# Attention of a two-layer diffusion block: key tiles taken two at a time from a written plan, with the maxima of two heads side by side on the rows of TensorE

## The chip, the core and the metric

The kernel runs as one program on one core of a Trainium2 chip. Its time is the device time of one execution in microseconds (us). Several executions are made, and their median is the number to compare.

A core has TensorE (PE, matrix products into PSUM), VectorE (DVE), ScalarE (ACT), GpSimd (POOL) and SyncE (SP, which issues most transfers). Each engine works through its own instructions in order and waits where an operand or a buffer isn't ready.

## The reference

Two layers over 1024 tokens (and, in the first layer, 256 context tokens) of width 1024: a mixer of attention, short convolution and a recurrent unit, and then 16 experts, each of which picks its own tokens. The change lies in the attention alone:

```
def gqa_attend(q, k, v):
    s = jnp.einsum('bqhgd,bkhd->bhgqk', q, k, preferred_element_type=jnp.float32) * (HEAD_DIM ** -0.5)
    p = jax.nn.softmax(s, axis=-1).astype(v.dtype)
    return jnp.einsum('bhgqk,bkhd->bqhgd', p, v)
...
    k_all = jnp.concatenate([k_ctx, k_lat], axis=1)      # 256 + 1024 keys
    att_x = lax.map(lambda qb: gqa_attend(qb, k_all, v_all), q_blocks)   # 8 blocks of 128 queries
...
    att_c = gqa_attend(q_ctx, k_ctx, v_ctx)              # first layer only: 256 queries, 256 keys
```

There are 8 query heads of 64 channels on 2 key heads (kv 0 and 1, four query heads each). All inputs are float32.

## The kernel before

Each layer has four stages: projections with convolution and recurrence, attention, output projection with routing, experts. The attention of a layer is a stretch of some 230 to 250 us, in which the order of every instruction on PE, ACT, DVE and POOL is the order of the code.

**Query tiles and steps.** A query tile has 128 tokens with all 8 heads. It runs over 10 key tiles of 128 keys, and each of these is one *step*; the two context tiles of the first layer run over 2. That is 84 steps in the first layer and 80 in the second. One step (`scores`, lines 887 to 904) does this for each kv: two products of 512 columns into a PSUM tile `St` (L893 with the high halves of q and k, L894 with the low halves and the shift), an exponential by ACT into `PT` (L896), and an addition of `PT` to the running sum `acc` (L904). `St` has two buffers and `PT` has eight. The additions go to POOL for kv 0, and for kv 1 while the key tile's number is under `JP` = 4; the others go to DVE. Then `weigh` (L911) multiplies `PT` with V into `O`, for both kv, two steps late (`LAG` = 2). Its two products stand in the two halves of TensorE's columns.

**Preparation of the next tile.** The exponential needs the negative maximum of each query and head as a shift, before the tile's first step. `q_prep` is a generator of 16 pieces for a tile: four transposes into a PSUM tile `X` (L747) with ACT copies of the high half (L753, L756) and DVE differences for the low half (L758); then for each pair of heads two pieces with 2 products of 512 columns and a DVE maximum over 1024 columns (L769, L771), and one with 2 products of 256 columns and a maximum over 512 (L778, L780); then the negative (L797, L798); then a transpose of it (L803) and two DVE products that put it into the low half of q (L805). `X` has two buffers of 1024 columns. `advance` deals these pieces out evenly, one or two behind each kv of the steps.

**Late work.** A list `late` counts steps (`tick`) and holds the sums' reciprocals (`norm`, L919, `norm2`), and the splitting of the output projection's weights into halves: 32 parts of 256 columns, an ACT copy (L862) and a DVE difference (L863) each. From step 36 on, `w_out_unit` loads one of four weight blocks; the parts of a block follow at every second tick, and the blocks overlap, so that there come to be two parts for two steps. In the first 8 steps of a layer `filler` puts in products of the modulation (L159).

Of the kernel before, what the change touches and what calls it, by code (L numbers as in the profile page):

```python
# [8 lines left out]
F32 = mybir.dt.float32  # L9
# [35 lines left out]
def dit_kernel(ctx: ExitStack, tc: tile.TileContext, x, c, ctxt, c_ctx, w_mod, b_mod, norm1_g, norm2_g,  # L45
# [157 lines left out]
    JP, LAG, NL, NL1, NL2, LD, PB = 4, 2, 3, 2, 4, 2, 8  # L203
# [64 lines left out]
    for l in range(layers):  # L268
# [474 lines left out]
        def q_prep(tt, slot, xb, joint):  # L743
            nk = NTA if tt >= NTC else NTC
            b = xb()
            for p_ in range(4):
                pe.transpose(b[0][:, p_ * P:(p_ + 1) * P], qraw[:, tt, p_ * P:(p_ + 1) * P], ident)  # L747
            qq = slot()
            qh, ql = qq[:, 0:1024], qq[:, 1024:2048]
            v = lambda t: t.rearrange("p (h a t) -> p a h t", a=2, t=P)  # L750
            src = b[0].rearrange("p (h t) -> p h t", h=4)
            for a in range(2):
                act.activation(v(qh[0:64])[:, a], src[a * 64:a * 64 + 64], AF.Copy)  # L753
            yield
            for a in range(2):
                act.activation(v(qh[64:128])[:, a], src[a * 64:a * 64 + 64], AF.Copy)  # L756
            for a in range(2):
                vec.tensor_sub(v(ql[64:128])[:, a], src[a * 64:a * 64 + 64], v(qh[a * 64:a * 64 + 64])[:, a].bitcast(F32))  # L758
            mx = at_mx()
            yield  # L760
            np_ = 0
            if nk == NTA:
                for p_ in range(4):
                    ks = kst[p_ // 2]
                    hs = (2 * p_, 2 * p_ + 1)
                    for h in hs:
                        b = xb()
                        for i in range(2):
                            pe.matmul(b[i], qh[:, h * P:(h + 1) * P], ks[:, i * 512:(i + 1) * 512], start=True, stop=True)  # L769
                        if joint:  # L770
                            vec.tensor_reduce(mx[:, h, 0:1], b[2], axis=AX.X, op=OP.max)  # L771
                        else:
                            for i in range(2):
                                vec.tensor_reduce(mx[:, h, 2 * i:2 * i + 1], b[i], axis=AX.X, op=OP.max)
                        yield
                    b = xb()
                    for i, h in enumerate(hs):
                        pe.matmul(b[0][:, i * 256:(i + 1) * 256], qh[:, h * P:(h + 1) * P], ks[:, 1024:1280],  # L778
                                  start=True, stop=True)
                    vec.tensor_reduce(mx[:, hs[0]:hs[1] + 1, 1], b[0].rearrange("p (h k) -> p h k", h=2), axis=AX.X,  # L780
                                      op=OP.max)
                    np_ = 2 if joint else 3
                    yield
            else:
                for kv in range(2):
                    b = xb()
                    for i in range(4):
                        h = 4 * kv + i
                        pe.matmul(b[i // 2][:, (i % 2) * 256:(i % 2) * 256 + 256], qh[:, h * P:(h + 1) * P],
                                  kst[kv][:, 0:256], start=True, stop=True)  # L790
                    vec.tensor_reduce(mx[:, 4 * kv:4 * kv + 4, 0], b[2].rearrange("p (h k) -> p h k", h=4), axis=AX.X,
                                      op=OP.max)
                    np_ = 1
                    yield
            nm = nmx[len(tiles) % 2]
            if np_ > 1:
                vec.tensor_reduce(nm[:, 0:8], mx[:, :, 0:np_], axis=AX.X, op=OP.max)  # L797
# [3 lines left out]
            yield  # L801
            b = xb()
            pe.transpose(b[0][0:HD, 0:P], nm, ident)  # L803
            for kv in range(2):
                vec.tensor_mul(ql[0:HD, kv * 512:(kv + 1) * 512].rearrange("p (h t) -> p h t", h=4),  # L805
                               b[0][0:HD, None, 0:P].to_broadcast([HD, 4, P]),
                               ident[0:HD, 4 * kv:4 * kv + 4, None].to_broadcast([HD, 4, P]))
            tiles[tt] = (qh, ql, nk)
            yield
# [15 lines left out]
        first = q_prep(NTC, rslot, xb1, False)  # L825
# [55 lines left out]
        def xb2():  # L881
            t = pps.tile([P, 1024], F32, name="X", tag="X", bufs=2)
            return t[:, 0:512], t[:, 512:1024], t
# [4 lines left out]
        def scores(tt, j, kv):  # L888
# [7 lines left out]
            act.activation(pt, st, AF.Exp)  # L896
            if j == 0:
                return
# [5 lines left out]
            eng.tensor_add(a, PT[tt, 0, kv] if first_ else a, pt)  # L904
# [33 lines left out]
        cost = lambda t2: 16 if t2 >= NTC else 6  # L938
        rest = [q_prep(t2, qslot if t2 >= NTC else rslot, xb2, True) for t2 in order[1:]]
# [6 lines left out]
        done = [0]  # L946

        def advance(target):
            while done[0] < target:
                while rest and next(rest[0], "end") == "end":  # L950
                    rest.pop(0)
                done[0] += 1
# [10 lines left out]
        base = st_n = 0  # L963
        advance(LD)
        for g in groups:
            n_p = sum(cost(order[i + 1]) for i in g if i + 1 < len(order))
            n_s = sum(2 * tiles[order[i]][2] if order[i] in tiles else 2 * NTC for i in g)
            slot_ = 0
            for tt in (order[i] for i in g):
                for j in range(tiles[tt][2]):  # L970
                    for kv in range(2):
                        scores(tt, j, kv)
                        if kv:
                            lag.append((tt, j))
                            while len(lag) > LAG:
                                a, b = lag.pop(0)
                                weigh(a, b)
                                if b == tiles[a][2] - 1:
                                    late.append([NL, lambda a=a: norm(a)])
                            tick()  # L980
                        slot_ += 1
                        advance(base + LD + n_p * slot_ // n_s)
                    filler(1)
                    st_n += 1
                    if st_n in WS:
                        w_out_unit(WS.index(st_n))
            base += n_p
# [668 lines left out]
```

## Time and profile before

| | us |
|---|---|
| median of 3 runs | 2744.03 (2739.17 to 2745.43) |
| profiled execution, its own time | 2740.52 |
| its span, first to last instruction | 2738.7 |
| attention of the first layer, first score to last sum of a tile | 311.5 to 560.3 |
| attention of the second layer, up to its last sum of a tile | 1757 to 1987 |

Over the whole span PE is busy 95% of the time, DVE 73%, ACT 54% and POOL 27%. These are averages over unlike stages; the change concerns the two attention stretches, together some 480 us, and has to be read there.

### The profile page before, as it was taken

How to read it: one execution, taken by the hardware profiler on the slowest of the kernel's cores; microseconds unless marked ns; L12 is line 12 of the kernel's file. 1: busy time of each engine (PE TensorE's matmuls, PEld its weight loads, DVE VectorE, ACT ScalarE, POOL GpSimd, SP SyncE). 2: the span in 40 equal slices, each digit the busy share in tenths (PEclk: the TensorE clock that was granted, in tenths of full speed). 3: DMA queues.
4: the chain of work that ended last, by engine and by line, in shares of the span. 5: the costliest groups of instructions: out<-in, count | busy, mean ns of one | idle time of the engine just before them, and what ended most of it. 6: DMA issues, size and time to landing. Idle time of an engine off the chain costs nothing. (4 is left out here: it accounts for less than half of the span.)

```text
span 2738.7 us, 35062 instructions
## 1 busy us (share of the span) xinstructions
PE 2592.2 (95%) x13475; PEld 1809.7 (66%) x13475; DVE 1985.9 (73%) x2172; ACT 1466.6 (54%) x1688; POOL 733.7 (27%) x722
## 2 busy tenths in 40 slices
PE   7999999999799999999998899999995999999996
PEld 5689644467466666666665679744474788777774
DVE  6735678755777777777775665678746998898886
ACT  5812255632356565665664662255522776766665
POOL 2003556612311211121111201556600211133323
PEclk9999999999899999999999999999998999999998
DMA  7410311144688888787787411310146899999995
GB/s 235 173 47 10 124 25 32 55 149 151 244 313 296 294 298 293 289 300 289 274 310 252 164 57 40 123 24 9 60 167 238 325 392 374 353 368 379 372 373 188
DMA packets 177341, 579.12 MB, mean 211 GB/s; under 512 B 19137, under 2 KB 46249, under 8 KB 172054
## 3 DMA queue, kind: packets, MB, share of 16 engines
q1 hardware_dynamic: 164438, 535.87, 52.9%
q0 software_dynamic: 12688, 41.00, 5.8%
q8 instruction: 106, 1.74, 0.3%
q14 instruction: 61, 0.50, 0.1%
q10 hardware_dynamic: 48, 0.01, 0.0%
HBM read 534.70 MB, written 42.07 MB: 211 GB/s over the span
## 5 line engine op out<-in xcount | busy, mean ns | idle before, releaser
L81 DVE TENSOR_TENSOR wlo<-raw,whi 128x2048 fp32r<-128x2048 f32 x399 | 899.4, 2286 | 172.0 <-ACT whi L81 169.7
L81 ACT ACTIVATE whi<-raw 128x2048 fp32r<-128x2048 f32 x399 | 751.9, 1915 | 316.6 <-DMA raw<-in_w_gate_dram 67.8
L896 ACT ACTIVATE PT<-St 128x512 f32<-128x512 f32 x328 | 189.1, 596 | 171.0 <-PE St L894 164.6
L1369 PE MATMUL pg<-whi,xx 128*128 128x512 f32 x1024 | 267.0, 403 | 5.5 <-DVE xx L1416 5.2
L1369 PE MATMUL pu<-whi,xx 128*128 128x512 f32 x1024 | 264.6, 400 | 1.1 <-ACT whi L81 1.1
L1369 PE MATMUL py<-whi,tt 128*128 128x512 f32 x1024 | 263.2, 399 | 1.4 <-ACT tt L1481 0.9
L904 POOL TENSOR_TENSOR acc<-acc,PT 128x512 f32<-128x512 f32 x160 | 205.0, 1290 | 143.0 <-ACT PT L896 142.6
L1369 PEld LDWEIGHTS py<-whi,tt 128*128 128x128 f32 x1024 | 191.6, 189 | 62.4 <-issue 7.5
L1369 PEld LDWEIGHTS pg<-whi,xx 128*128 128x128 f32 x1024 | 190.8, 190 | 62.1 <-issue 11.7
L1369 PEld LDWEIGHTS pu<-whi,xx 128*128 128x128 f32 x1024 | 190.5, 189 | 56.3 <-issue 12.6
L1538 POOL DMA_INDIRECT xd<-yo,ixx x16 | 43.5, 2720 | 529.2 <-DVE yo L1537 529.2
L911 PE MATMUL O<-PT,V 128*64 128x512 f32 x656 | 176.0, 617 | 0.0
L771 DVE TENSOR_REDUCE mx<-X 128x1 f32<-128x1024 f32 x112 | 135.3, 1218 | 24.1 <-PE X L769 23.6
L893 PE MATMUL St<-qq,kst 128*128 128x512 f32 x328 | 142.5, 434 | 3.7 <-ACT PT L896 3.3
L1369 PE MATMUL py<-wlo,tt 128*128 128x512 f32 x512 | 141.3, 398 | 3.5 <-DVE wlo L81 3.5
L1369 PE MATMUL pu<-wlo,xx 128*128 128x512 f32 x512 | 142.2, 399 | 1.4 <-DVE wlo L81 1.4
L1369 PE MATMUL pg<-wlo,xx 128*128 128x512 f32 x512 | 142.1, 400 | 0.2 <-DVE wlo L81 0.2
L904 DVE TENSOR_TENSOR acc<-acc,PT 128x512 f32<-128x512 f32 x96 | 106.6, 1111 | 39.0 <-ACT PT L896 38.1
L894 PE MATMUL St<-qq,ksu 128*128 128x512 f32 x328 | 130.6, 398 | 0.1
L1377 PE MATMUL pc<-raw,xcT 128*32 128x512 f32 x1024 | 116.5, 595 | 0.0
L1369 PEld LDWEIGHTS py<-wlo,tt 128*128 128x128 f32 x512 | 95.4, 189 | 28.3 <-DVE wlo L81 7.6
L1369 PEld LDWEIGHTS pu<-wlo,xx 128*128 128x128 f32 x512 | 97.0, 190 | 25.4 <-DVE wlo L81 2.7
(404 smaller groups left out, 4250.3 us busy)
## 6 DMA issues: line engine op xcount, KB each, us to landing
raw<-in_w_gate_dram SPq DMA_DIRECT2D x128, 1024.0 KB
raw<-in_w_up_dram SPq DMA_DIRECT2D x128, 1024.0 KB
raw<-in_w_down_dram SPq DMA_DIRECT2D x128, 1024.0 KB
rawm<-in_w_mod_dram SPq DMA_DIRECT2D x24, 1024.0 KB
raw<-in_w_mod_dram SPq DMA_DIRECT2D x24, 1024.0 KB
raw<-in_w_in_dram SPq DMA_DIRECT2D x15, 1024.0 KB
xd<-x SPq DMA_DIRECT2D x16, 512.0 KB
h2d<-h SPq DMA_DIRECT2D x16, 512.0 KB
```

The lines of the kernel that those rows point to most:

```text
L81: parts = (lambda: act.activation(hi, raw, AF.Copy), lambda: vec.tensor_sub(lo, raw, hi.bitcast(F32)))
L771: vec.tensor_reduce(mx[:, h, 0:1], b[2], axis=AX.X, op=OP.max)
L893: pe.matmul(st, kst[kv][:, ks], qh[:, cs], start=True, stop=False)
L894: pe.matmul(st, kst2[kv][:, ks], ql[:, cs], start=False, stop=True)
L896: act.activation(pt, st, AF.Exp)
L904: eng.tensor_add(a, PT[tt, 0, kv] if first_ else a, pt)
L911: pe.matmul(Os[tt][kv * 64:(kv + 1) * 64, :], V[:, j, kv * 64:(kv + 1) * 64], PT[tt, j, kv], start=(j == 0), stop=(j == nk - 1))
L1369: pe.matmul(ps[:, n * 512:(n + 1) * 512], a[:, k, :], b[:, kk, n * 512:(n + 1) * 512], start=(u == 0 and i == 0 and kk == 0), stop=(u == 3 ...
L1377: pe.matmul(pc[32 * g:32 * g + 32, :], xc(2 * u + kk), raw[:, kk, n * 512:(n + 1) * 512], start=(u == 0), stop=(u == 3))
L1538: pool.indirect_dma_start(out=xd[l], out_offset=bass.IndirectOffsetOnAxis(ap=ixx[:, e:e + 1], axis=0), in_=yo, in_offset=None, compute_op= ...
```

## The change

The steps are now taken in *cycles* of two. A cycle emits the scores of both steps one behind the other (four `St` tiles), and then two weighings in a row: the second step of the cycle before, and the first step of this one. The sums for kv 0 come ahead of the weighings and those for kv 1 behind them, and `JP` is 6 instead of 4: of the nine additions for kv 1 of a tile, POOL now does five and DVE four (before three and six). The generator with `advance` is gone. In its place a dictionary `plan` names what of the next tile's preparation stands at each of seven places of each cycle: M, E, F behind the second, third and fourth score pair, H between the weighings, A and B behind them.

```diff
-    JP, LAG, NL, NL1, NL2, LD, PB = 4, 2, 3, 2, 4, 2, 8
+    JP, NL, NL1, NL2, PB = 6, 3, 2, 4, 8
...
+            def unit(self, p_, i, rows):
+                o, n = ((0, 512), (512, 512), (1024, 256))[i]
+                b = xb2()
+                for a in range(2):
+                    h = 2 * p_ + a
+                    r = slice(64 * a, 64 * a + 64) if rows else slice(0, P)
+                    ks = (kst2 if rows and a else kst)[p_ // 2]
+                    pe.matmul(b[:, a, :n], self.qh[r, h * P:(h + 1) * P], ks[r, o:o + n], start=True, stop=True)
+                vec.tensor_reduce(self.mx[:, 2 * p_:2 * p_ + 2, i], b[:, :, :n], axis=AX.X, op=OP.max)
...
+        TA = ((0, "B"), (1, "M"), (1, "E"), (1, "F"))
...
+                qx = mine[0] if mine else None
+                seq = []
+                for p_ in range(4):
+                    seq += [(p_, "A", p_, 0), (p_, "B", p_, 1), (p_ + 1, "M", p_, 2)]
+            if qx:
+                for d, place, p_, i in seq:
+                    put(c0 + d, place, u(qx, p_, i, place != "M"))
+                put(last, "M", qx.neg)
+                put(last, "H", qx.shift)
+                nxt = g[-1] + 1
+                if nxt < len(preps):
+                    turned(preps[nxt], last, TA)
...
-                while len(lag) > LAG:
...
-                        advance(base + LD + n_p * slot_ // n_s)
...
+        for c_ in range(len(steps) // 2):
+            two = steps[2 * c_:2 * c_ + 2]
+            for half in range(2):
+                for kv in range(2):
+                    scores(*two[half], kv)
+                    if half or kv:
+                        do(c_, "MEF"[2 * half + kv - 1])
+                lag.append(two[half])
...
+            summed(*two[0], 0)
+            summed(*two[1], 0)
+            tick()
+            filler(2)
+            while len(lag) > 1:
+                a, b = lag.pop(0)
+                weigh(a, b)
+                if len(lag) == 2 or c_ == 0:
+                    do(c_, "H")
...
+            summed(*two[0], 1)
+            summed(*two[1], 1)
+            tick()
+            do(c_, "A")
+            do(c_, "B")
```

`unit` makes the maxima of two heads over the same 512 keys (places A and B) as *row-tiled* products: head a of the pair contracts 64 rows only, the first head on partitions 0 to 63 (`kst`), the second on partitions 64 to 127 (`kst2`, which holds a copy of the same high halves there). Each goes to its own 512 columns of `X`. So these maxima are of the high half of k alone, and before they were of the high and the low half together on all 128 rows; the maximum serves only as a shift, which cancels in the softmax. At place M the 256 remaining keys are done as before, on 128 rows. The first four cycles of a tile end with A and B; the fifth ends with the four transposes of the tile after next. The negative stands at M and the shift at H of the fifth cycle, and the copies of the high half lie between the exponentials of the first cycle of the tile that follows.

On PE, in the second tile of the second layer, a stretch of two steps stood like this (`kst` and `ksu` are the keys, `O` the weighing, `X` the maxima, `St` the scores):

```order
L911 MATMUL O<-PT,V 64x512 x2
L769 MATMUL X<-kst_12816,qq 128x512 x2
L893 MATMUL St<-qq,kst_12815 128x512
L894 MATMUL St<-qq,ksu_13878 128x512
L893 MATMUL St<-qq,kst_12816 128x512
L894 MATMUL St<-qq,ksu_13879 128x512
L911 MATMUL O<-PT,V 64x512 x2
L778 MATMUL X<-kst_12816,qq 128x256 x2
L893 MATMUL St<-qq,kst_12815 128x512
L894 MATMUL St<-qq,ksu_13878 128x512
L769 MATMUL X<-kst_12816,qq 128x512 x2
L893 MATMUL St<-qq,kst_12816 128x512
```

The same place is now one cycle, from the second row-tiled unit (B) to the two weighings:

```order
L912 MATMUL X<-kst_12815,qq 128x512
L912 MATMUL X<-ksu_13878,qq 128x512
L938 MATMUL St<-qq,kst_12815 128x512
L939 MATMUL St<-qq,ksu_13878 128x512
L938 MATMUL St<-qq,kst_12816 128x512
L939 MATMUL St<-qq,ksu_13879 128x512
L912 MATMUL X<-kst_12815,qq 128x256 x2
L938 MATMUL St<-qq,kst_12815 128x512
L939 MATMUL St<-qq,ksu_13878 128x512
L938 MATMUL St<-qq,kst_12816 128x512
L939 MATMUL St<-qq,ksu_13879 128x512
L958 MATMUL O<-PT,V 64x512 x4
```

A weighing stood between every two score pairs and their successors; now four score pairs stand in a run with only the 256-key unit among them, and four V products stand together.

On DVE, in a late tile of the second layer in which the weights of the output projection are split, the stretch of the sixth to tenth step stood like this (`mx` are the maxima, `acc` the sums, `wlo` the weights' low halves):

```order
L904 TENSOR_TENSOR acc_15106<-acc_15106,PT 128x512
L863 TENSOR_TENSOR wlo<-raw,whi 128x256 x2
L771 TENSOR_REDUCE mx<-X 128x1
L904 TENSOR_TENSOR acc_15106<-acc_15106,PT 128x512
L927 RECIPROCAL r_15163<-r_15163 128x8
L780 TENSOR_REDUCE mx<-X 128x2
L771 TENSOR_REDUCE mx<-X 128x1
L904 TENSOR_TENSOR acc_15106<-acc_15106,PT 128x512
L863 TENSOR_TENSOR wlo<-raw,whi 128x256 x2
L771 TENSOR_REDUCE mx<-X 128x1
L780 TENSOR_REDUCE mx<-X 128x2
L904 TENSOR_TENSOR acc_15106<-acc_15106,PT 128x512
```

In the same tile, from the third cycle's end to the fifth's, it now stands like this:

```order
L974 RECIPROCAL r_15163<-r_15163 128x8
L913 TENSOR_REDUCE mx<-X 128x2 x3
L860 TENSOR_TENSOR wlo<-raw,whi 128x256 x2
L951 TENSOR_TENSOR acc_15110<-acc_15110,PT 128x512 x2
L913 TENSOR_REDUCE mx<-X 128x2 x3
L759 TENSOR_REDUCE nmx_12819<-mx 128x8
L760 TENSOR_SCALAR nmx_12819<-nmx_12819 128x8
L860 TENSOR_TENSOR wlo<-raw,whi 128x256 x2
L768 TENSOR_TENSOR qq<-X,identr 64x512 x2
L951 TENSOR_TENSOR acc_15110<-acc_15110,PT 128x512 x2
```

Sums, low halves and maxima took turns one by one; now two low halves and two sums stand in a block ahead of the maxima of A and B, and two low halves stand between the negative and the shift.

## Rows read from the trace of the kernel before

**Rows 1.** Windows over the second layer's attention: us, busy (x instructions) by engine, PEclk, DMA

```profile
1757.00:1987.00 230.00, 226.71 (x939) 100.59 (x937) 174.67 (x214) 126.16 (x233) 132.08 (x103) 1.00 0.15 48
```

**Rows 2.** Windows from sum to sum of a tile: one without, three with weight splitting

```profile
1803.28:1831.25 27.97, 27.82 (x116) 13.08 (x114) 22.10 (x25) 15.06 (x26) 16.59 (x14) 1.00 0.03 11
1887.19:1915.69 28.50, 28.14 (x115) 13.00 (x113) 25.34 (x33) 17.49 (x34) 16.82 (x14) 1.00 0.04 10
461.24:489.69 28.45, 28.10 (x116) 13.01 (x114) 25.47 (x35) 18.22 (x36) 16.83 (x14) 1.00 0.14 47
489.69:518.48 28.79, 28.20 (x115) 12.99 (x113) 25.95 (x36) 18.11 (x36) 16.79 (x14) 1.00 0.15 47
```

**Rows 3.** Timeline of PE: start, us, engine, line, operation; a step without maxima

```profile
444.44 1.08 PE L911 MATMUL O<-PT,V 128*64 128x512 f32 x4
445.45 0.50 PE L893 MATMUL St<-qq,kst 128*128 128x512 f32 x1
445.78 0.39 PE L894 MATMUL St<-qq,ksu 128*128 128x512 f32 x1
...
446.25 0.39 PE L894 MATMUL St<-qq,ksu 128*128 128x512 f32 x1
446.56 1.08 PE L911 MATMUL O<-PT,V 128*64 128x512 f32 x4
```

**Rows 4.** Timeline of PE where three weighings stand in a row, and a tile's sum

```profile
556.56 2.79 PE L911 MATMUL O<-PT,V 128*64 128x512 f32 x12
559.29 1.05 PE L919 MATMUL St<-acc,on 128*32 128x512 f32 x4
```

**Rows 5.** Timeline of PE at the transposes of a tile

```profile
448.35 0.60 PE L747 MATMUL X<-identr,qraw 128*128 128x128 f32 x4
448.70 0.48 PE L893 MATMUL St<-qq,kst 128*128 128x512 f32 x1
```

**Rows 6.** Timeline: exponentials behind scores, and scores that wait for one

```profile
315.63 1.08 ACT L896 ACTIVATE PT<-St 128x512 f32<-128x512 f32 x2
316.28 0.50 PE L893 MATMUL St<-qq,kst 128*128 128x512 f32 x1 [0.43 <-ACT PT L896]
316.62 0.40 PE L894 MATMUL St<-qq,ksu 128*128 128x512 f32 x1
...
446.27 1.09 ACT L896 ACTIVATE PT<-St 128x512 f32<-128x512 f32 x2 [1.06 <-PE St L894]
```

**Rows 7.** Timeline: maxima behind their products, and a product behind DVE

```profile
437.17 0.73 PE L769 MATMUL X<-kst,qq 128*128 128x512 f32 x2
437.94 1.23 DVE L771 TENSOR_REDUCE mx<-X 128x1 f32<-128x1024 f32 x1
...
1850.15 1.39 DVE L758 TENSOR_TENSOR qq<-X,qq 64x512 fp32r<-64x512 f32 x2
1851.69 0.70 PE L769 MATMUL X<-kst,qq 128*128 128x512 f32 x2
```

**Rows 8.** Groups of the second layer's attention: xcount, busy us, mean ns, idle before

```profile
L911 PE MATMUL O<-PT,V 128*64 128x512 f32 x320 | 85.9, 617 | 0.0
L771 DVE TENSOR_REDUCE mx<-X 128x1 f32<-128x1024 f32 x56 | 67.8, 1219 | 13.9 <-PE X L769 13.6
L904 DVE TENSOR_TENSOR acc<-acc,PT 128x512 f32<-128x512 f32 x48 | 55.0, 1147 | 21.5 <-ACT PT L896 20.9 <-issue 0.3
L780 DVE TENSOR_REDUCE mx<-X 128x2 f32<-128x512 f32 x28 | 18.9, 676 | 11.6 <-PE X L778 11.6
L863 DVE TENSOR_TENSOR wlo<-raw,whi 128x256 fp32r<-128x256 f32 x32 | 15.5, 509 | 5.9 <-ACT whi L862 5.8
L862 ACT ACTIVATE whi<-raw 128x256 fp32r<-128x256 f32 x32 | 12.1, 413 | 2.4 <-DMA raw<-in_w_out_dram 2.4
```

**Rows 9.** Timeline: a sum on DVE beside one on POOL

```profile
1844.90 1.28 POOL L904 TENSOR_TENSOR acc<-acc,PT 128x512 f32<-128x512 f32 x1 [1.10 <-ACT PT L896]
1845.28 1.45 DVE L904 TENSOR_TENSOR acc<-acc,PT 128x512 f32<-128x512 f32 x1 [0.65 <-ACT PT L896]
```

More of the change, by code (lines that the diff above doesn't have):

```diff
@@ L945, in dit_kernel, with put, turned, do @@
                 groups[-1].append(i)
[L946 to L952, printed above, removed]
+        preps = [Prep(t2) for t2 in order[1:]]
+        plan = {}
+        def put(c_, place, f_):
+            plan.setdefault((c_, place), []).append(f_)
+        def turned(q, c_, places):
+            for (d, place), f_ in zip(places, (q.turn, q.low, q.copy3, q.copy4)):
+                put(c_ + d, place, f_)
+        TA = ((0, "B"), (1, "M"), (1, "E"), (1, "F"))
+        TM = ((0, "M"), (0, "E"), (0, "F"), (0, "A"))
+        u = lambda q, p_, i, rows: lambda: q.unit(p_, i, rows)
+        c0 = 0
+        for gi, g in enumerate(groups):
+            n_c = sum((NTA if order[i] >= NTC else NTC) // 2 for i in g)
+            mine = [preps[i] for i in g if i < len(preps)]
+            last = c0 + n_c - 1
+            if len(g) > 1:
+                qc, qx = mine
+                for kv in range(2):
+                    put(c0, "AB"[kv], lambda q=qc, kv=kv: q.cunit(kv))
+                put(c0 + 1, "M", qc.neg)
+                put(c0 + 1, "H", qc.shift)
+                turned(qx, c0 + 1, TM)
+                seq = [(1, "B", 0, 0)]
+                for p_ in range(3):
+                    seq += [(p_ + 2, "M", p_, 2), (p_ + 2, "A", p_, 1), (p_ + 2, "B", p_ + 1, 0)]
+                seq += [(5, "M", 3, 1), (5, "M", 3, 2)]
+            else:
+                qx = mine[0] if mine else None
+                seq = []
+                for p_ in range(4):
+                    seq += [(p_, "A", p_, 0), (p_, "B", p_, 1), (p_ + 1, "M", p_, 2)]
[7 more added lines that the diff above has]
+                    turned(preps[nxt], last, TA)
+            c0 += n_c
+        def do(c_, place):
+            for f_ in plan.pop((c_, place), ()):
+                f_()
         lag = []
@@ L961, in tick @@
                 late.pop(0)[1]()
[L963 to L974, printed above, removed]
[L975 to L987 removed]
+        for f_ in (preps[0].turn, preps[0].low, preps[0].copy3, preps[0].copy4):
+            f_()
+        steps = [(tt, j) for tt in order for j in range(NTA if tt >= NTC else NTC)]
+        st_n = 0
+        for c_ in range(len(steps) // 2):
+            two = steps[2 * c_:2 * c_ + 2]
+            for half in range(2):
+                for kv in range(2):
+                    scores(*two[half], kv)
+                    if half or kv:
+                        do(c_, "MEF"[2 * half + kv - 1])
+                lag.append(two[half])
+                st_n += 1
+                if st_n in WS:
+                    w_out_unit(WS.index(st_n))
+            summed(*two[0], 0)
[7 more added lines that the diff above has]
+                    do(c_, "H")
+                if b == tiles[a][2] - 1:
+                    late.append([NL, lambda a=a: norm(a)])
+            summed(*two[0], 1)
[3 more added lines that the diff above has]
+            do(c_, "B")
         while lag:
```

145 lines of the change are left out of this document (81 added, 64 removed).

## The prediction, made before the changed kernel ran

> **What bounds the kernel now.** I read the windows over the attention first: PE is busy for 226.7 of 230 us at the full clock (1.00), DVE for 174.7 [rows 1]. So a tile takes what PE's stream takes. From one sum to the next a tile without weight splitting needs 27.97 us, 27.82 of them busy on PE and 22.1 on DVE; three tiles with splitting need 28.50, 28.45 and 28.79 (mean 28.58) with 25.3 to 26.0 on DVE [rows 2]. PE does the same work in both, so the 0.6 us are lateness of DVE.
>
> PE's prices come from its timeline, from start to start. Two products of 512 columns take 0.47 (445.78 to 446.25), so 0.23 each. A weighing takes 1.01 (444.44 to 445.45) [rows 3]; three in a row take 2.73 (556.56 to 559.29), so each further one costs 0.86, and leaving V costs 0.15 [rows 4]. The first score behind V takes 0.33 instead of 0.23 (0.10 more), and the last one 0.31 before V (0.08) [rows 3]. A visit to V therefore costs 0.33 beyond its stream, and a step without maxima is 4 x 0.23 + 0.86 + 0.33 = 2.11 (444.44 to 446.56 is 2.12).
>
> **What the edits do, one by one.**
>
> *Two weighings in a row* save one visit in each of the 42 + 40 cycles: 0.33 x 82 = 27 us. The price is paid by the scores. `St` has two buffers, so the third score pair of a run has to wait for the first exponential. That starts 0.49 behind the second half of its pair (446.27 behind 445.78 [rows 3, 6]), lasts 0.60 (two in 1.08, 0.49 apart), and the next product follows 0.05 after its end (315.63 + 0.60, 316.28): 1.14 in all. PE itself would be there after 3 x 0.23 = 0.69. So 0.45 is lost where nothing stands between, and the first product after a wait takes 0.34 [rows 6], another 0.1. Before, a weighing of 1.01 lay between. What is saved at V is lost here unless place M fills it.
>
> *Row-tiled maxima.* Sixteen full products of a tile, 3.7 us, become eight pairs. No row shows two row tiles. Bounds: 0.23 for a pair if both run side by side, 0.46 if not. The nearest row is V, whose two column halves do: 320 records of 617 ns are 197 us of records in 85.9 us of busy time [rows 8]. I take 0.23, and for entering and leaving what V's columns cost (0.10, 0.15; bounds 0 and 0.33 each).
>
> *M behind A.* `X` has two buffers: A takes one, B the other, and the M unit of the next cycle needs A's again. I walk one cycle from A's first product at 0. A 0.33, B 0.23, leaving 0.15: scores 1 at 0.71 and 0.94, scores 2 at 1.17 and 1.40, PE free at 1.63. The maximum of A starts 0.04 after its products' end (437.17 + 0.73, 437.94; the first product behind a change has a record of 0.50), so at 0.54, and ends at 1.76 (1.22 [rows 8]). A product follows DVE by 0.15 (1850.15 + 1.39, 1851.69) [rows 7]: M at 1.91, a wait of 0.28. M ends at 2.24; the first exponential was done at 0.94 + 1.14 = 2.08. Scores 3 and 4 end at 3.16, V starts at 3.25, lasts 1.72, leaving 0.15: the next A at 5.12. So M fills the hole behind the exponential but finds DVE's instead. Entering or leaving row tiles for nothing changes little, as M waits for DVE anyway.
>
> *The first cycle of a tile* has four transposes (0.35 [rows 5]) ahead of it and no M: scores at 0.35, the copy of the high half ahead of the first exponential, scores 3 only at 1.90, the next A at 4.88. *The shift* between the weighings costs a second visit, 0.33; a tile's sum about 1.0 [rows 4].
>
> *DVE in the fourth cycle.* The two sums for kv 1 now stand in a block ahead of A's maximum. The last maximum and M's end at 3.64 (2.96 + 0.68); the sums take 1.15 each [rows 8], so they end at 5.94, and A's maximum was due at 5.12 + 0.54 = 5.66: M is 0.28 later. The negative follows in time for the shift. Two sums fewer (`JP`) relieve DVE by 2.3 per tile. POOL gets two more: 16.6 + 2.6 = 19.2 of 27 [rows 2], and in the second and third cycle four sums of 1.28 [rows 9] in 5.12. That is just covered, as eight `PT` buffers hold two cycles; I take nothing, and each 0.1 by which POOL's four were longer would cost 0.2 per tile.
>
> A plain tile: 4 x 5.12 + 4.88 + 0.33 + 1.0 + 0.28 = 27.0 against 27.97, so **-1.0 for each of 8 tiles** (those with a preparation and without two parts in a cycle).
>
> *Tiles with splitting.* `tick` now runs at two places of a cycle, and both parts come to its end. ACT copies them behind the fourth exponential, which ends at 4.05: 4.46, 4.87 (0.41 each); DVE's low halves (0.51 each) end at 5.51 [rows 8]. In the first three cycles A's maximum (5.66) just escapes. In the fourth the two sums stand behind the low halves: 5.51 + 2.30 = 7.81, so A's maximum is 2.15 late, and M waits for it with everything behind it on PE. In the fifth two low halves stand between the negative and the two shift products, and the next tile's first scores need these: I count 0.5. The sums, the low halves of q and two parts more make the first A of that tile 0.6 late. With 2.15 in the place of 0.28: 26.7 + 2.15 + 0.5 + 0.6 = 30.0 against 28.58: **+1.4 for each of 6 tiles**. Before, single sums and parts stood between the maxima and were caught up within a step.
>
> *The last tile of each layer* has no preparation: a cycle is 0.33 + 3 x 0.23, the wait of 0.45 with its 0.1, two more pairs, 1.72 and the changes, 4.46 against 2 x 2.12: +0.22, ten times 2.2. The two context tiles I take at nothing; a cycle each, at most 1 us either way. The loads of the weights and the modulation's products keep their steps.
>
> Sum: -8.0 + 8.4 + 2.2 = +3. The profiled execution at 2740.5 would be 2743.5; the median of the runs lies 3.5 above it. **2747 us.**
>
> The Trainium skill has a measured price for row tiles (TensorE: Matmul & The Clock Gate, Part 3, measured speedup vs the span model): four row tiles of 512 columns gave 3.07 times the speed, not four. As an estimate from that page, a pair would be 0.23 x 4/3.07 = 0.30; A's maximum and with it M would come 0.07 later in four cycles of 14 tiles, +4 us. No run here shows it, and the sum above does without it.
>
> **The rivals.**
>
> *DVE catches up (faster).* If the low halves don't hold up A's maximum, because ACT takes the parts earlier or DVE has slack, all 14 tiles gain: the six take 27.0 instead of 28.58, so -8.0 - 9.5 + 2.2 = -15: 2729. For it: DVE is free for 2.8 to 3.2 us even in these tiles [rows 2]. Against it: the order puts parts, sums and maxima in one block behind the last exponential. It decides where A's maximum in the fourth cycle starts under 0.5 late.
>
> *Row tiles don't overlap (slower).* At 0.46 a pair, scores 1 start at 1.17, the first exponential frees scores 3 only at 2.54, and A comes again at 5.52: +0.40 in four cycles, 1.6 in each of 8 plain tiles and, as DVE is late there anyway, perhaps half in the six: +17.6 on top of +3, 2765. Nothing in the trace speaks against it but V's columns.
>
> *DVE slower in blocks (slower).* A sum on DVE beside one on POOL took 1.45, not 1.15 [rows 9]. POOL now works more, and next to these sums. Two sums and the two pairs of parts longer by 0.3 each are 1.3 in each of six tiles, +8: 2755.
>
> *The merge brings nothing, or more.* Were ACT's release of `St` quicker than 1.14, cycles without M would gain; these are few, and the others wait for DVE. This stays within the first case.
>
> **Chances.** Gains and losses cancel to about +3 (2740 to 2755): 0.44. DVE catches up, wholly or half: 0.25. Row tiles one behind the other: 0.13. Slower DVE: 0.12. Something not listed: 0.06. From no change a measurement can tell about 0.2%, 5.5 us. Of the first case 0.05 falls below 2738.5, 0.22 within and 0.17 above 2749.5; of the second 0.21 below and 0.04 within; the third and the fourth lie above but for 0.03 within; the rest is split. So faster 0.28, same 0.31, slower 0.41. The range reaches from the second case to the third, 2728 to 2765; the likeliest case's own is 2740 to 2755.
>
> **What would show it.** In the profile after: plain tiles from sum to sum at 27.0 and those with splitting at 30; PE's idle time before the 256-column `X` products released by DVE's maximum, some 0.3 in a plain cycle and over 1 us in the fourth cycle of a tile with splitting; idle time before every third score pair of a last tile released by an exponential; the two row-tiled products of a pair starting together and the next pair 0.23 later; DVE busy some 4 us less for two tiles. Wrong would be: pairs 0.46 apart, M without a wait, or tiles with splitting as short as the others.

## The result, and the profile after

The changed kernel takes **2779.22 us** (median of 4 runs, 2777.34 to 2780.24), the kernel before 2744.73 on the same chip: ratio **1.0129** (95% interval 1.0112 to 1.0147), slower by 35 us. The forecast was 2747, its range ended at 2765. The profiled execution's span is 2775.5, 36.8 more than before. From the first score to ACT's copy of the last tile's sums, the first layer's attention takes 19.5 longer and the second's 16.1: nearly all of it lies there.

Windows of the kernel after, columns as in [rows 1, 2]: the second layer's attention (with some 18 us ahead of its first score at 1774.75), two plain tiles, two with splitting, and at the end one of the first layer and two stretches of it.

```profile
1757.00:2024.00 267.00, 236.30 (x1051) 107.11 (x1050) 178.75 (x222) 129.32 (x242) 168.82 (x131) 0.97 0.18 59
1825.78:1854.91 29.13, 27.05 (x115) 11.86 (x113) 19.95 (x23) 14.49 (x26) 19.20 (x16) 1.00 0.04 10
1854.91:1883.79 28.88, 26.82 (x115) 11.80 (x114) 19.73 (x23) 14.50 (x26) 19.36 (x16) 1.00 0.04 10
1913.26:1944.86 31.60, 27.30 (x116) 11.81 (x114) 24.20 (x32) 17.39 (x35) 19.64 (x16) 1.00 0.03 9
1944.86:1977.12 32.26, 27.20 (x116) 11.82 (x114) 26.64 (x34) 17.38 (x35) 19.73 (x16) 1.00 0.22 74
466.68:501.75 35.07, 30.03 (x116) 12.78 (x114) 27.81 (x35) 17.79 (x36) 21.80 (x17) 0.91 0.11 38
...
478.00:494.00 16.00, 12.89 (x55) 5.38 (x52) 12.83 (x19) 8.86 (x19) 7.29 (x6) 1.00 0.21 74
494.00:501.75 7.75, 6.75 (x19) 2.60 (x17) 5.26 (x7) 3.16 (x7) 4.75 (x4) 0.58 0.00 1
```

PE did get less to do: 26.8 to 27.1 busy in a plain tile against 27.82 [rows 2]. But it was idle for 0.15 of the plain tile before, and is for 2.1 now, and for 4.3 to 5.1 of one with splitting. What it waits for, over the second layer's attention (total us, times, longest; before, over the stretch of [rows 1], the same list had 1.4, 0.8 and 0.4 in all):

```profile
PE X L912 <- DVE mx L913: 8.4, 8, 1.3
PE St L938 <- ACT PT L941: 5.8, 9, 3.7
PE X L912 <- ACT qq L745: 5.3, 6, 0.9
PE X L766 <- DVE nmx L760: 4.8, 6, 0.8
```

Each of these four lines stands for a cause of its own; of the second, one wait of 3.7 is most. The places, in timelines (start, us, engine, line):

```profile
1841.08 1.26 POOL L951 TENSOR_TENSOR acc<-acc,PT 128x512 f32<-128x512 f32 x1 [0.20 <-ACT PT L941]
1841.11 1.27 DVE L760 TENSOR_SCALAR nmx<-nmx 128x8 f32<-128x8 f32 x1
1842.52 0.27 PE L766 MATMUL X<-identr,nmx 128*64 128x128 f32 x1 [0.78 <-DVE nmx L760]
...
1848.11 0.59 ACT L745 ACTIVATE qq<-X 64x512 fp32r<-64x512 f32 x1 [0.84 <-DVE qq L749]
1849.99 0.49 PE L912 MATMUL X<-kst,qq 64*128 64x512 f32 x1 [0.88 <-ACT qq L745]
...
1949.55 5.36 POOL L951 TENSOR_TENSOR acc<-acc,PT 128x512 f32<-128x512 f32 x4 [0.26 <-ACT PT L941]
1950.24 2.31 DVE L860 TENSOR_TENSOR wlo<-raw,whi 128x256 fp32r<-128x256 f32 x2 [0.90 <-ACT whi L859]
1952.58 2.90 DVE L913 TENSOR_REDUCE mx<-X 128x2 f32<-128x1024 f32 x3
1953.80 0.50 PE L912 MATMUL X<-kst,qq 128*128 128x256 f32 x2 [0.95 <-DVE mx L913]
...
1777.82 1.20 ACT L745 ACTIVATE qq<-X 64x512 fp32r<-64x512 f32 x2 [1.49 <-DVE qq L749]
1780.33 1.08 ACT L941 ACTIVATE PT<-St 128x512 f32<-128x512 f32 x2
1780.98 0.79 PE L938 MATMUL St<-qq,kst 128*128 128x512 f32 x1 [3.71 <-ACT PT L941]
```

The first group: a negative of 128x8 numbers takes 1.27 and ends with the POOL sum beside it; the shift waits for it. Before, in a plain tile, it took 0.17 (at 1844.46), between one POOL sum that had ended at 1843.80 and the next from 1844.90 [rows 9]. The second: ACT's third copy of q waits for the low halves, and B, whose buffer the copies read, for the copies. The third: POOL does four sums in a row, two low halves of w_out beside them take 2.31, A's maximum starts 1.0 late (A's product stood at 1951.00, and in a plain tile the maximum starts 0.54 behind it, at 1832.47 behind 1831.93), and M waits. The fourth: at the layer's start the four copies of q, with a wait for the low halves between them, stand ahead of the first exponential, and PE has nothing but scores that wait for it.

The groups on DVE in the same stretch show who became dearer: the low halves 837 ns against 509, the negative 1209 against 311 (the last line is of the kernel before), while a sum, dear before at 1147 [rows 8], takes 865.

```profile
L951 DVE TENSOR_TENSOR acc<-acc,PT 128x512 f32<-128x512 f32 x32 | 27.7, 865 | 1.2
L860 DVE TENSOR_TENSOR wlo<-raw,whi 128x256 fp32r<-128x256 f32 x32 | 25.9, 837 | 29.9 <-ACT whi L859 29.9
L760 DVE TENSOR_SCALAR nmx<-nmx 128x8 f32<-128x8 f32 x7 | 8.5, 1209 | 0.2
...
L798 DVE TENSOR_SCALAR nmx<-nmx 128x8 f32<-128x8 f32 x7 | 2.2, 311 | 0.2
```

### The profile page after: what moved, and what is told of

Same layout as the page of the kernel before. It is cut to its first block, busy times and chain, and to the rows that moved or that the text cites. A ratio compares the mean times of both kernels' runs of the same rounds, so it can differ in the third digit from the quotient of the medians.

```text
span 2775.5 us, 34968 instructions
## 1 busy us (share of the span) xinstructions
PE 2585.7 (93%) x13475; PEld 1797.0 (65%) x13475; DVE 1972.7 (71%) x2140; ACT 1459.7 (53%) x1688; POOL 781.3 (28%) x754
## 5 line engine op out<-in xcount | busy, mean ns | idle before, releaser
L951 POOL TENSOR_TENSOR acc<-acc,PT 128x512 f32<-128x512 f32 x192 | 251.1, 1319 | 105.3 <-ACT PT L941 101.8
L941 ACT ACTIVATE PT<-St 128x512 f32<-128x512 f32 x328 | 181.5, 596 | 177.2 <-PE St L939 168.9
L913 DVE TENSOR_REDUCE mx<-X 128x2 f32<-128x1024 f32 x168 | 165.8, 1038 | 77.3 <-PE X L912 76.2
L958 PE MATMUL O<-PT,V 128*64 128x512 f32 x656 | 165.4, 617 | 0.0
L1633 POOL DMA_INDIRECT xd<-hy,ixx x15 | 50.7, 3380 | 234.0 <-DVE hy L1632 234.0
```

The source lines that it names most:

```text
L913: vec.tensor_reduce(self.mx[:, 2 * p_:2 * p_ + 2, i], b[:, :, :n], axis=AX.X, op=OP.max)
L951: eng.tensor_add(a, PT[tt, 0, kv] if first_ else a, PT[tt, j, kv])
L958: pe.matmul(Os[tt][kv * 64:(kv + 1) * 64, :], V[:, j, kv * 64:(kv + 1) * 64], PT[tt, j, kv], start=(j == 0), stop=(j == nk - 1))
L1633: pool.indirect_dma_start(out=xd[l], out_offset=bass.IndirectOffsetOnAxis(ap=ixx[:, e:e + 1], axis=0), in_=yo, in_offset=None, compute_op= ...
```

## The experiments

All ratios are to the kernel before, on the same chip, 95% interval behind. The tile times are from one copy of the sums on ACT to the next (read from each profile's timeline), for the second layer: three plain tiles, three intervals with splitting (the last of them reaches into the last tile), the rest of the last tile.

| kernel | ratio | plain | splitting | last |
|---|---|---|---|---|
| before | 1 | 28.03 27.96 27.98 | 28.50 29.11 25.28 | 15.89 |
| after | 1.0129 | 29.18 28.88 29.47 | 31.59 32.26 29.86 | 15.68 |
| e1 no negative | 1.0118 (1.0102-1.0133) | 28.36 28.02 28.63 | 33.09 32.18 29.75 | 15.69 |
| e2 low behind | 1.0168 (1.0152-1.0184) | 29.90 30.80 30.80 | 33.24 33.94 30.09 | 15.67 |
| e3 full rows | 1.0149 (1.0135-1.0163) | 29.65 29.33 29.40 | 31.87 32.53 30.13 | 15.67 |
| e4 sums spread | 1.0086 (1.0072-1.0100) | 29.17 28.85 29.44 | 30.44 30.51 27.67 | 16.74 |
| e5 three edits | 1.0036 (1.0024-1.0048) | 27.74 27.42 28.30 | 29.66 29.75 27.43 | 16.74 |
| e6 pool all | 1.0080 (1.0067-1.0093) | 27.48 27.45 27.90 | 30.56 31.25 29.24 | 19.30 |
| e7 before, rows | 1.0032 (1.0023-1.0040) | 28.62 28.58 28.58 | 28.88 28.87 25.55 | 15.88 |
| e8 sum first | 1.0093 (1.0080-1.0106) | 27.48 27.43 28.19 | 31.08 32.77 31.38 | 16.16 |
| e9 low behind B | 1.0037 (1.0024-1.0051) | 27.51 27.44 27.46 | 28.20 36.38 29.07 | 16.16 |
| e10 start | 1.0013 (1.0004-1.0022) | 27.78 27.43 28.32 | 29.67 29.72 27.43 | 16.73 |
| e11 all | 1.0019 (1.0010-1.0029) | 27.48 27.43 27.41 | 28.20 34.82 28.07 | 15.63 |
| e12 all, full rows | 1.0093 (1.0077-1.0108) | 28.78 28.75 28.72 | 29.48 34.57 28.34 | 15.63 |
| e13 loads early | 0.9981 (0.9972-0.9990) | 27.48 27.41 27.86 | 28.20 28.73 29.10 | 15.62 |
| e14 only low behind B | 1.0090 (1.0076-1.0104) | 28.90 28.88 28.88 | 29.41 34.64 27.26 | 15.68 |
| e15 no low halves | 1.0046 (1.0032-1.0059) | 28.35 28.86 28.89 | 29.18 28.86 26.70 | 15.68 |
| e16 JP 4 | 1.0127 (1.0111-1.0142) | 28.34 28.92 29.50 | 32.14 35.45 30.07 | 15.69 |

**What the low halves of w_out cost (e15, e14).**

```
-  vec.tensor_sub(l_[:, c], raw[:, c], h_[:, c].bitcast(F32))        # e15; l_ is a zero tile
+  behind.append(lambda: vec.tensor_sub(l_[:, c], ...))              # e14
   do(c_, "A"); do(c_, "B")
+  while behind: behind.pop(0)()
```

> The changed kernel without the low halves of w_out: DVE doesn't work them out, and a tile of zeros, set once per layer on POOL, stands in their place in the products after the attention. It prices them: if they are what makes splitting tiles longer than plain ones, seven tiles fall by 2 to 3 to the plain 29.2, -15 to -20: ratio 1.005 to 1.008. If ACT's copies or the sums make the difference: 1.010 to 1.013.

> The changed kernel with one edit: the low halves of w_out behind B's maximum, so that neither of the cycle's maxima stands behind them. My prediction's term (the low halves put A's maximum off, by 2.15 in a splitting tile's fourth cycle): the splitting tiles go from 31.6 to 32.3 down to 30.0 to 30.5, less where the load of w_out comes late: ratio 1.006 to 1.010. Rival B (DVE's sums in blocks beside POOL are the larger part, and the low halves only fill the time): 1.011 to 1.014.

Without them the splitting tiles are plain tiles (29.18, 28.86), and the ratio falls by 0.0083: **23 of the 35 us are theirs** (give or take 6, by the two intervals), more than expected, and the wait for a maximum is gone from the second layer's list. Moved behind B (e14), the first splitting tile is 29.41, about as without them, and PE's wait for a maximum falls from 8.4 to 1.3; the next tile is 34.64 for another reason (e13). So it is not that DVE has too much to do: it is what they stand ahead of.

**Sums in blocks, and JP (e4, e16).**

```
-  eng = pool if kv == 0 or j < JP else vec
+  eng = pool if kv == 0 or j % 2 else vec        # e4;  e16: JP = 4
```

> The changed kernel with DVE's four sums of a tile spread over its cycles: POOL takes those of the odd key tiles, DVE those of the even ones, so each cycle has one sum on DVE instead of none in the first three and two in the last two. The counts of both engines stay. Theory A (DVE's work stands in blocks ahead of A's maximum, and M waits for that): M's waits of about 1 us in the last cycles of the six splitting tiles fall to some 0.3, -2 a tile, and 0.3 in the others: 2763 to 2768. Rival D (what lengthens DVE's work is POOL working beside it, wherever it stands): 2776 to 2784.

> The changed kernel with JP back at 4: kv 1's sums of the key tiles 4 and 5 on DVE instead of POOL, in the third cycle, six sums of a tile on DVE and twelve on POOL. Theory L (what costs time is DVE work that meets POOL's): POOL's stretch of four sums ends sooner in the third cycle, but two more sums stand ahead of A's maximum there: plain tiles +0.3, splitting ones +1 to +2: ratio 1.016 to 1.020. If POOL's two more sums were the trouble, this would undo it: 1.008 or less.

e4 gained 12 us, as theory A said, with equal counts on both engines: splitting tiles 30.4 instead of 31.6 and 32.3. Plain tiles gained nothing: no maximum had been late there. The reason in the splitting ones is seen in its timeline: POOL's odd sum now waits for DVE's even one, so DVE works alone then, and its sum takes 0.68 (the row puts the wait down to the reciprocal that stands on DVE right behind that sum).

```profile
1938.08 0.68 DVE L951 TENSOR_TENSOR acc<-acc,PT 128x512 f32<-128x512 f32 x1
1938.91 2.53 POOL L951 TENSOR_TENSOR acc<-acc,PT 128x512 f32<-128x512 f32 x2 [1.37 <-DVE r L974]
```

e16 missed both ways: in time, to have six sums on DVE or four is the same.

**The small work (e1, e2, e5).** The sign goes into `sel`; the low halves of q behind the fourth copy; and in e5, with both the sign and the sums spread as in e4, another order of the copies (c10 is the copy of rows 64 to 127 for the even heads, low1 the low half for the odd ones; a bar separates the places).

```
+  vec.tensor_scalar(sel, sel, -1.0, None, op0=OP.mult)              # e1, once per layer
-  vec.tensor_scalar(nm[:, 0:8], nm[:, 0:8], -1.0, None, op0=OP.mult)
   copies and low halves: c00 | c11 low0 low1 | c01 | c10            # after
                          c00 | c11 | c01 | c10 low0 low1            # e2
                          c00 | c01 low0 | c11 low1 | c10            # e5
```

> The changed kernel, but the maxima go to the shift unnegated, and the sign sits in the vector sel, made once per layer: the small multiplication by -1 on DVE ahead of each shift (1.27 us where a sum runs on POOL) is gone. Theory A (small DVE work, stretched beside POOL and queued behind others, holds PE up): the wait of the shift's transpose, 0.78 in nearly each of 14 tiles, goes; 2779 becomes 2766 to 2769. Rival B (the merged run of scores is held by the two St buffers, so that a wait which goes here comes back at the next exponential): 2776 to 2779, with the shift's wait replaced by one for ACT.

> The changed kernel, with the two low halves of the next tile's q behind its fourth copy instead of between the second and the third. Theory A: ACT's third copy no longer waits 0.84 for DVE, the fourth exponential of a tile's first cycle comes sooner, and B's row-tiled product of that cycle loses its wait of 0.88: about -0.9 in each of 13 tiles, 2767 to 2770. Rival B: the low halves now stand ahead of A's maximum on DVE in that cycle, M waits for it instead, and the time stays at 2777 to 2782.

> Three edits of the changed kernel together: no negative on DVE, DVE's sums spread over the cycles, and a new order of the four copies of q (rows 0 to 63 first, then 64 to 127), with one low half behind the second copy and one behind the third, so that only the second of them can hold up a copy, by some 0.15 instead of 0.84. Theory A (each of these waits of PE is its own, and goes for good): the shift's 0.8 in 14 tiles and B's 0.7 of 0.88 in 13 come off the time with sums spread alone (ratio 1.0086): -20, ratio 1.001 to 1.003. Rival B (DVE as a whole is too slow in the splitting tiles, so that a wait removed in one place comes back at the next maximum): plain tiles at 27.6, splitting ones still at 30, ratio 1.005 to 1.007.

e1: plain tiles fell by 0.82 to 0.86, the shift's wait, and nothing came in its place there. In the splitting ones the wait came back behind the shift: the low half of the next tile's scores now waits for the shift's products on DVE (0.94 in two of them), and the wait for a maximum stayed at 8.4; in the tile of 33.09 the clock fell besides (0.68 from 1938 to 1942). A is right for the plain tiles, and in the others a wait came back, though on DVE and not on ACT as B said. The 3 us in all lie within the noise. e2 fell through: ACT has four copies and four exponentials without a break in that cycle, the low halves came last of all, and B waited longer than before:

```profile
1880.58 0.59 ACT L745 ACTIVATE qq<-X 64x512 fp32r<-64x512 f32 x1
1881.21 1.39 DVE L749 TENSOR_TENSOR qq<-X,qq 64x512 fp32r<-64x512 f32 x2 [3.67 <-PE X L912]
1882.74 0.46 PE L912 MATMUL X<-kst,qq 64*128 64x512 f32 x1 [1.58 <-DVE qq L749]
```

e5, one low half behind each copy that it needs, left B a wait of 0.28. Two of its three plain tiles (27.74, 27.42) beat those before; its splitting ones stayed at 29.7, as B expected.

**Does DVE wait for POOL? (e8, e6).** Both stand on e5: e8 puts DVE's sum ahead of the low halves, e6 all sums on POOL (`JP = 10`).

```
   summed(*two[0], 0); summed(*two[1], 0)
+  summed(*two[0], 1)                             # e8
   tick()
...
-  summed(*two[0], 1)
   summed(*two[1], 1)
```

> The kernel with three edits, and DVE's one sum of a cycle stands ahead of the low halves of the weights (whose copy on ACT comes behind the fourth exponential) instead of behind them. Theory A: DVE does the sum while it would wait for ACT, the low halves end 0.68 earlier and A's maximum with them: M's waits of 0.4 to 1.0 in the splitting tiles halve, -1 a tile in six, ratio 0.002 below the kernel with three edits. Rival L (the sum ahead now collides with POOL's sums and waits up to 1.3 for them): no change or +0.002.

> As the kernel with three edits, but all 18 sums of a tile on POOL, none on DVE. Theory L (a DVE operation with two inputs in SBUF waits while a POOL operation runs; maxima, which read PSUM, don't): plain tiles lose their last waits for a maximum (27.3), and in splitting tiles the low halves of weights each wait for a POOL sum, up to 1.3 us, so that these tiles stay at 29 to 30: ratio 1.000 to 1.006. Rival P (POOL, with 18 x 1.28 + 1.27 = 24.3 us of work in 27.5, becomes the bound, the PT buffers run out and exponentials wait for POOL): over 1.009.

Theory A failed in e8, and the rival L undershot: splitting tiles became 31 to 33. Without DVE's sum to wait for, POOL did its sums one behind the other, and each of two low halves waited for one:

```profile
1938.12 3.02 POOL L951 TENSOR_TENSOR acc<-acc,PT 128x512 f32<-128x512 f32 x2 [0.39 <-ACT PT L941]
1938.80 2.62 DVE L860 TENSOR_TENSOR wlo<-raw,whi 128x256 fp32r<-128x256 f32 x2 [0.22 <-ACT whi L859]
```

Alone a low half takes 0.41. Two in 2.62 are two POOL sums long, and POOL's two sums are longer by about one low half (3.02 against 2.53): they take turns. In e6 plain tiles are as short as the shortest (27.45, DVE 14.85 busy) and splitting ones at 31; the ratio fell between the two theories, and both hold in part, as its last tile took 19.30, where the sum waits for POOL.

**The start of a layer (e10, on e5).**

```
-  for f_ in (preps[0].turn, preps[0].low, preps[0].copy3, preps[0].copy4): f_()
+  preps[0].turn()
+  for place, f_ in zip("MEF", (preps[0].low, preps[0].copy3, preps[0].copy4)):
+      plan.setdefault((0, place), []).insert(0, f_)
```

> The kernel with three edits, and of the first prepared tile of a layer only the transposes and one copy stand ahead of the first cycle; the other copies and low halves come behind its first score pairs, as in the other tiles. Theory S (a part of the loss has nothing to do with the tiles: at each layer's start ACT does four copies and waits for low halves ahead of the first exponential, and PE waits 3.7 for it): the wait of the third score pair falls to 1 or less, -2 to -3 in each layer: ratio 1.0010 to 1.0022. Rival (the wait moves to A's product, which needs all four copies): no change, 1.0036.

As theory S said: 1.0036 to 1.0013, 6 us for two layers, with no tile behind it changed. The third score pair waits for 0.36 instead of 3.7:

```profile
1758.81 0.80 PE L938 MATMUL St<-qq,kst 128*128 128x512 f32 x1 [0.36 <-ACT PT L941]
```

**Low halves behind B on e5, and all together (e9, e11, e13).** e11 is e5 with the edits of e10 and e14 and the last tile's kv 1 sums on DVE; e13 has `WS = (34, 42, 52, 60)` for `(36, 44, 52, 60)` besides.

> The kernel with three edits (ratio 1.0036), and the low halves of w_out are emitted behind B's maximum instead of at the ticks, so that on DVE they stand behind both maxima of a cycle; ACT's copies stay. Theory A (they hold up A's maximum, and M waits for that): M's waits of 0.43, 0.41 and 1.46 in a splitting tile go, B's maximum and M's own have slack: -1.2 to -1.5 in each of seven tiles, ratio 0.9995 to 1.001. Rival L (wherever they stand, each waits up to 1.3 us for a POOL sum, and something behind them is late): 1.003 to 1.006, with waits of A's or B's products for M's or A's maximum instead.

> The kernel with three edits, and with both further edits (low halves of w_out behind B, copies of the first tile behind its scores), and all of kv 1's sums of the last tile on DVE. Theory A: the gains add up: -9, -5 and -1.5 from 1.0036: ratio 0.997 to 0.999, faster than both kernels. Rival B (DVE and POOL bound the splitting tiles): 1.001 to 1.003.

> The kernel with all edits, and the first two loads of w_out a cycle earlier (steps 34 and 42 instead of 36 and 44). Theory R (behind B, the last low half of a unit gives its raw buffer back later; the load of the unit after the next starts later, ACT's copy of the first part waits 4.3 for it, and behind that copy, on ACT, stand the exponentials): that wait and the tile of 34.8 in the second layer and of 30.5 in the first go to 28.2: -7 to -9, ratio 0.9985 to 0.9995. Rival B (these tiles are long because DVE and POOL have too much to do): 1.001 to 1.003.

e9 and e11 missed in an instructive way: in e11 every splitting tile went to 28.2 as expected, but for one in each layer (30.47 and 34.82). A unit's last low half gave `raw` back later, the load of the unit after the next began later, and ACT, in order, kept exponentials behind the copy:

```profile
1926.01 0.42 ACT L859 ACTIVATE whi<-raw 128x256 fp32r<-128x256 f32 x1 [4.28 <-DMA raw<-in_w_out_dram]
1926.96 0.74 PE L938 MATMUL St<-qq,kst 128*128 128x512 f32 x1 [2.03 <-ACT PT L941]
```

e13 shows that this was it: with the first two units a cycle earlier that tile is 28.73 (and 28.32 in the first layer; the interval behind it, with a wait of 1.84 for the negative, became 29.10 from 28.07), and the kernel, at 2737.48, is **faster than both** (0.9981), by as little as can be told apart. Its windows of a plain and two splitting tiles:

```profile
1828.37:1855.78 27.41, 26.82 (x115) 11.86 (x115) 17.61 (x22) 14.47 (x27) 19.71 (x16) 1.00 0.03 10
1883.64:1911.84 28.20, 26.87 (x115) 11.84 (x115) 25.94 (x31) 17.21 (x35) 19.23 (x15) 1.00 0.07 21
1911.84:1940.57 28.73, 27.06 (x115) 11.91 (x115) 25.78 (x31) 17.20 (x35) 20.19 (x16) 1.00 0.20 73
```

DVE is busy for 25.9 there, as in the slow tiles of the kernel after (24.2, 26.6): the same work, at places where nobody waits for it.

**Row tiles (e3, e7, e12).**

```
-  put(c0 + d, place, u(qx, p_, i, place != "M"))
+  put(c0 + d, place, u(qx, p_, i, False))        # e3 on after, e12 on e11
```

> The changed kernel with its row-tiled products undone: both products of A's and B's units on all 128 rows, one behind the other. If row tiling saves what the walk of one cycle gave (0.40 a cycle, 1.6 a tile of 14, half of it where DVE is late), this costs 16 to 22 us: 2795 to 2801. Rival C (the row tiles' changes of mode are part of the loss): 2779 or less.

> The kernel before with the row-tiled maximum products alone: both heads of a pair side by side for two blocks of 512 keys, and the block of 256 on all rows; order, merges and sums as before. On PE a unit becomes one pair of 0.23 with entering and leaving instead of two products of 0.47. If entering and leaving cost 0.25 together, as I took from V's columns: ratio 0.998 to 1.002. If they cost the 0.10 that the changed kernel's trace shows (0.33 a pair): -0.14 x 8 in 16 tiles where PE is the bound, ratio 0.993 to 0.996. Rival C (row-tiled products cost more than they save): 1.003 or more.

> The kernel with all edits, but with the row-tiled products undone, both on all 128 rows. By the rows of the changed kernel, A, B and the first score behind them take 0.33 + 0.33 + 0.33, and would take 0.47 + 0.47 + 0.24, +0.2 a cycle, and A's maximum is due 0.14 later: +0.8 to +1.2 in each of 14 tiles where PE is the bound, ratio 0.004 to 0.006 above the kernel with all edits. Rival C (changes of mode eat up what row tiling saves, as it did alone in the kernel before): 0.000 to 0.002 above, or below it.

e3 cost some 5 us, not 16, and its interval overlaps that of the kernel after: there most of what row tiles save is lost in waits, and a part is hidden by the clock, which fell in two tiles of the kernel after and in none of e3 (last section). e12 shows their worth where PE is the bound: 28.75 against 27.43, 1.32 a tile or 0.33 a cycle, a little more than expected (0.0074 of the whole). Put into the kernel before, one pair at a time between score pairs, they cost 0.6 a plain tile: rival C. A pair has 0.09 ahead of it (1838.79 + 0.23 to 1839.11), lasts to the next score 0.44, and that score takes 0.33 instead of 0.23: 0.63, against 0.47 for two full products. Eight of these would be 1.3 a tile; the loss is smaller as some pairs stand behind V, where a pair and the score behind it take 0.76 (1841.22 to 1841.98) against 0.80 with full products before (1807.09 to 1807.89).

```profile
1838.79 0.40 PE L907 MATMUL St<-qq,ksu 128*128 128x512 f32 x1
1839.11 0.49 PE L771 MATMUL X<-kst,qq 64*128 64x512 f32 x1
1839.12 0.50 PE L771 MATMUL X<-ksu,qq 64*128 64x512 f32 x1
1839.55 0.50 PE L906 MATMUL St<-qq,kst 128*128 128x512 f32 x1
```

## Why the prediction was wrong

**Right: PE's stream.** A cycle with A, B and M was walked at 5.12 and takes 5.16 where nothing else is late (A at 1852.83 and 1858.00 in e1 are 5.17 apart); the first cycle, 4.88, took 4.89 to A (1843.73 to 1848.62); the last tile's cycle, 4.46, takes 4.50 (535.02 to 539.52 in e11). M stands 1.83 behind A (1854.66 in e1), walked 1.91. The tile of 27.0 is 27.4 in e11. The products of a pair run side by side, as assumed, and the next pair follows 0.34 behind the first:

```profile
1831.93 0.50 PE L912 MATMUL X<-kst,qq 64*128 64x512 f32 x1
1831.93 0.50 PE L912 MATMUL X<-ksu,qq 64*128 64x512 f32 x1
1832.27 0.39 PE L912 MATMUL X<-kst,qq 64*128 64x512 f32 x1
1832.27 0.39 PE L912 MATMUL X<-ksu,qq 64*128 64x512 f32 x1
1832.59 0.50 PE L938 MATMUL St<-qq,kst 128*128 128x512 f32 x1
```

A + B came to 0.66 and the score behind to 0.34; I had 0.33, 0.23 and 0.15 ahead of scores, 0.71 in all.

**Wrong, the step that failed: the splitting tiles.** "DVE's low halves (0.51 each) end at 5.51. In the first three cycles A's maximum (5.66) just escapes." The margin was 0.15, and 0.51 was a mean in an order in which POOL paused in between. Beside four POOL sums in a row two took 2.31, so A's maximum did not escape in other cycles either; M waited about 1 us again and again. Forecast +1.4 in six tiles, 8.4 in all; measured in the seven intervals +3.1, +3.2, +4.6 and (first layer) +4.2, +6.8, +3.8, +3.3, **28.9 of 35.6**. Some 2.6 of these are the last tiles' longer cycles (4.50 against 2 x 2.12, ten of them), and a few us the falls of the clock in the first layer. The fourth cycle, where I saw most of the loss (2.15), I had too high: two sums behind the low halves took 1.41 (1957.42 in the second layer), not 2.30, and M waited 1.12 there. The rival "DVE slower in blocks" named the mechanism and its place, but priced it at 0.3 an operation, +8.

The Trainium skill has the rule that I passed by (SBUF — State Buffer, Who interferes with whom): DVE operations with two inputs in SBUF, or in a two-port mode, which it says `tensor_scalar` can enter, share a pair of ports with GpSimd as an exclusive lock (those with two inputs against a GpSimd operation that reads SBUF), so that the later one waits for the whole instruction of the other; those with one input outside these modes don't. The traces agree: the negative ends with the POOL sum (1.27, and 0.17 with POOL idle), low halves and sums take turns with POOL's (2.62 for two), a sum alone takes 0.68 and 1.45 beside POOL [rows 9], while maxima, which read PSUM, stay at 1.22.

**Wrong: "The negative follows in time for the shift."** I gave it no price; it took 1.27; the shift waited 0.78. e1 takes 0.8 a plain tile off.

**Missed: a shared tile.** I walked the first cycle as far as A and let B follow. It waits 0.88 for copies that wait for low halves of other columns of `qq`.

**Missed: the start of a layer.** I priced the tiles alone. The first tile's copies stood ahead of the first exponential before, too; but they came without a wait for low halves (1.49 now), and PE had a unit of maxima and the modulation's products between the second and the third score pair. These now stand behind the fourth, and PE waits 3.71 (second layer). The stretch up to the first tile's sums became 1.7 and 1.9 longer; e10 gets 6 us back, more than was lost.

So a plain tile was +1.2 in the second layer and +0.3 in the first, not -1.0: waits of 0.8 and 0.9, both brought on by DVE, took more than the 0.8 to 1.0 that PE saved. **Mis-sized:** the last tiles (+2.2 forecast) ended 0.2 sooner each, with their longer cycles inside the intervals above. Moving two more sums from DVE to POOL, taken at nothing, made no difference in time (e16).

What stays open: the parts do not add up singly (e1's 3, e4's 12, e15's 23 and e10's 6 are 44, of 35 and of PE's gain), as a wait removed in a splitting tile partly comes back as another, and as the clock differs between them (below); e15 bounds the low halves only together with the blocks that they share.

## What to carry to other kernels

Where operations of two engines take turns, price an operation by what the other engine does at that moment in the new order, not by its mean in the old one; a small operation can cost as much as the other engine's large one. When steps are set in blocks, ask of each block who waits for what stands behind it, and put work for which nobody waits behind the maxima that gate PE; then ask which buffer it gives back later, and which load starts later for that. Row tiles pay when several stand in a run, and cost when one stands alone among full products.

## What was not expected of the hardware

The granted clock fell within tiles. In the stretch from 494 to 501.75 it was 0.58 in the mean, with most products at the lower of the two levels; in the 16 us ahead of it, at 1.00, PE had been busy for 12.89. The four V pairs of that cycle took 3.68 instead of 1.94, and the tile 35.07. The profiled executions of e4, e5, e10 and e15, with fewer waits, have no such fall inside a tile; e3's, with as many waits but all products on full rows, has none either; but e12's, on full rows too, has two, each behind a wait of PE of 2.2. So neither the number of waits nor the row tiles alone decide it; what does, no run here tells. At the layers' start, where PE waits longest, the clock was at the lower level from 1773 to 1785 (0.50), up to 10 us behind the first score; before, it had risen some 4 us behind it (1758).

Read in windows of 4 us over both attention stretches, the clock adds up to some 32 us at the lower level after the change, against 8 before; 22 of the 32 lie at the layers' starts and 10 in two tiles of the first layer. As an estimate from these, half the speed costs at most half of the 24 us more, 12 of the 35 us, and less where PE waits anyway. It came with the waits, and no run separates the two. The second layer's tiles show the loss without it: from the first tile's sums to the end they are 14.2 us longer, at a clock of 1.00. And it blurs small differences: e4's profiled execution had a mean clock of 0.976 over its whole span and took 2759.26, its other four 0.972 or 0.973 and 2763.26 to 2765.37.
